# A split-fp32 decoder trunk on one core: queries, keys, attention outputs and the residual stream transposed by DMA instead of on TensorE

## The chip, the cores and the metric

The kernel runs on one core of a Trainium2 chip. The metric is device time in microseconds for one launch, the median of several runs.

## The reference

Two pre-norm layers work on 256 positions of width 2048. Cut to what matters:

```
for layer in range(2):
    xn = rms_norm(h, norm_mix)                 # h: (256, 2048)
    proj = xn @ w_in                           # 2048 x 5656: q, k, v of both head groups, gates
    o = concat(nsa_attention(...),             # 8 heads: compressed, selected and window branch
               stick_breaking_attention(...))  # 8 heads: a = exp(log_sigmoid(z) + reverse cumsum)
    h = h + (rms_norm_per_head(o) * g_grp) @ w_out
    xn = rms_norm(h, norm_ffn)
    h = h + (silu(xn @ w_gate) * (xn @ w_up)) @ w_down
return rms_norm(h, norm_final)
```

All weights and activations are float32.

## The kernel before

The weights are the bulk of the work. A planner (`plan`) writes them down once as a fixed sequence of 402 items per layer, each 128 partitions by at most 1024 columns, and the main loops go through that sequence item by item. For item `pos` a loop does three things: `step(active)` advances every piece of side work by one stage, `prefetch(pos)` lets SyncE load raw weights five tiles ahead and splits the item three places ahead into two fp32r halves (`hi` on ScalarE, L166; `lo` = raw − hi on VectorE, L167; four buffers each), and `mm(pos)` issues the item's matmuls on TensorE (L409). Each product is three passes: xh·hi, xl·hi, xh·lo. A usual item is two k-tiles by 512 columns, twelve matmuls. The item's number is thus the only clock of the program order: an instruction's place on each engine's in-order queue is the item at which its generator reached that stage.

The side work is Python generators, each `yield` of which means "one item later". `qk_chunk` takes a finished projection of queries or keys (two tiles `nat`, rows = positions), transposes them on TensorE into PSUM (L616) and copies them out on ScalarE (L617). `sb_unit` does one block of stick-breaking attention: scores `z` on TensorE, three ScalarE operations on `e`, three VectorE operations that end in `c` (L771, L773, L774), `c` = exp(c) on ScalarE (L776), then four transposes of `c` on TensorE (L780), `aT` on VectorE, and the matmuls with `sv` (L797). `nsa_unit` has a similar chain, with `pT` copied out of PSUM on ScalarE (L664). `o_norm` writes the normalised attention output `on[c]`. `xt_gen` and `xt_block` turn 512 columns of positions-by-features into the transposed and split operand `xh`/`xl`: eight TensorE transposes (L374), two VectorE multiplications by the norm's gain (L376), ScalarE `xh` (L381), VectorE `xl` (L384). They do it for the attention output (`XO`, four blocks), for the FFN's input (`X`) and for the next layer's input.

`gated`, the FFN's product, is already transposed by DMA: ScalarE copies the two tiles `sil` apart into 16-bit planes `pl` (L923), a DMA transpose, issued from ScalarE's queue, moves `pl` to `plt` (L926), four ScalarE copies put the planes together again as `sT` (L934), and `ah`/`al` are the split operand of w_down (L938, L939). The four-item pause before `sT` is written into the generator, as is one `yield` after each `pl`:

```
nc.scalar.dma_start(pt.rearrange("p t b (a s) -> p (t b a) s", a=4),
                    pl.rearrange("p t b n -> p (t b n)"), transpose=True)
for _ in range(4):
    yield
```

Of the kernel before, what the change touches and what calls it, by code (L numbers as in the profile page):

```python
# [122 lines left out]
def trunk(ctx: ExitStack, tc: tile.TileContext, x, positions, cst, gT, gfin, bgate, posT, w2, ws, out):  # L123
# [58 lines left out]
    def spawn(g):  # L182
        active.append(g)
# [5 lines left out]
    def step(lst):  # L189
        for g in list(lst):  # L190
            try:
                next(g)
            except StopIteration:
                lst.remove(g)
# [26 lines left out]
    def quad(c):  # L221
        return slice(512 * c, 512 * c + 512)
# [137 lines left out]
    def new_x():  # L360
        return [None] * 4
# [26 lines left out]
    def tmp512(name="scr"):  # L388
        return tmpp.tile([P, 512], F32, tag="scr", name=name, bufs=3)

    def xt_gen(X, c, srcs, g, ready=None):
        if ready is not None:
            while ready not in flags:
                yield
        xt_alloc(X, c)
        xt_block(X, c, srcs, g)
        yield
# [43 lines left out]
    for l in range(DEPTH):  # L441
        g_mix, g_grp, g_ffn = gt[:, 3 * l, :], gt[:, 3 * l + 1, :], gt[:, 3 * l + 2, :]
        flags.clear()
        with ExitStack() as actx:
# [152 lines left out]
            def qk_chunk(name, accs):  # L597

                sc = rq if name[0] == "q" or name[:2] == "sq" else r
                ns = []  # L600
                for t in range(2):
                    n = nat()
                    evac(n, accs[t], t, sc)
                    ns.append(n)
                yield
                if name[0] != "s":
                    for t in range(2):
                        rope(ns[t].rearrange("p (n d) -> p n d", n=4), rt, t)
                        yield
                    yield  # L610
                dst = big(name)
                dv = dst.rearrange("p (n s) -> p n s", n=4)
                for t in range(2):
                    pt = tmp_ps()
                    for j in range(4):
                        T.transpose(pt[:, j * P:(j + 1) * P], ns[t][:, j * P:(j + 1) * P], ident)  # L616
                    A.activation(dv[:, :, t * P:(t + 1) * P], pt.rearrange("p (n s) -> p n s", n=4), AF.Copy)  # L617
                    yield
                big_t[name] = dv
                flags.add(name)  # L620
# [181 lines left out]
            def sb_driver(b):  # L802
                yield from wait_for("nsa", f"sq{b}", f"sk{b}")
                yield from pipeline([sb_unit(b, 0, [0, 1, 2, 3]), sb_unit(b, 1, [0, 1]), sb_unit(b, 1, [2, 3])], 2)

            spawn(prep())
            spawn(nsa_driver())
            spawn(sb_driver(0))
            spawn(sb_driver(1))
# [1 line left out]

            ocmp = {}
            accs = None
            XO = new_x()
            while seq[pos][1].mat in ("w_in", "w_cmp_k1", "w_cmp_v1"):
                it = seq[pos][1]
                if l == 0 and pos < 6:
                    prefetch(pos)
                    step(active)
                    if pos == 3:  # L820
                        late_loads()
                else:
                    step(active)
                    prefetch(pos)
                if it.mat == "w_in":
                    for kt in it.kts:
                        while X[kt // 4] is None:
                            step(active)
                    if it.first:
                        accs = [acc(), acc()]  # L830
                    mm(pos, accs, lambda kt: X[kt // 4])
                    if it.last:
                        nm = it.name
                        if nm in ("ck", "cv"):
                            spawn(c_chunk(nm, accs))
                        elif nm == "v" or nm[:2] == "sv":
                            spawn(v_chunk(nm, accs))
                        else:
                            spawn(qk_chunk(nm, accs))
                    if it.name == "sv1" and it.kts[-1] in (3, 7, 11):  # L840
                        c = it.kts[-1] // 4
                        spawn(xt_gen(XO, c, lambda t, c=c: on[c][:, t], g_grp, f"on{c}"))
                else:
                    nm = "ck" if it.name == "wk" else "cv"
                    while nm not in flat:
                        step(active)
                    if it.first:
                        ocmp[nm] = o_ps()
                    cmp_mm(pos, ocmp[nm], flat[nm])
                    if it.last:  # L850
                        flags.add(it.name)
                        spawn(c_tail(nm, ocmp[nm]))
                parts.pop(pos)
                pos += 1
# [21 lines left out]
            while seq[pos][1].mat == "w_out":  # L876
                it = seq[pos][1]
                step(active)
                prefetch(pos)
                if it.first:  # L880
                    accs[it.name] = [acc(), acc()]
                if XO[it.kts[0] // 4] is None:
                    while f"on{it.kts[0] // 4}" not in flags:
                        step(active)
                    need(XO, it.kts[0] // 4)
                    step(active)
                    step(active)
                mm(pos, accs[it.name], lambda kt: XO[kt // 4])
                c = int(it.name[1])
                if it.last:  # L890
                    spawn(h_add(accs[it.name], c, norm))
                if c == 3 and it.kts[-1] in (1, 5, 9, 15):
                    q = it.kts[-1] // 4
                    spawn(xt_gen(X, q, lambda t, q=q: h[:, t, quad(q)], g_ffn, f"h{q}"))
                parts.pop(pos)
                pos += 1


        with ExitStack() as fctx:
# [14 lines left out]
            def gated(c, accs):  # L914


                for t in range(2):
                    s = sil[c, t]
                    V.scalar_tensor_tensor(s, accs[t], r[:, t:t + 1], s, op0=OP.mult, op1=OP.mult)  # L919
                yield  # L920
                pl = fp.tile([P, 2, 2, 512], U16, tag="pl", name="pl", bufs=1)
                for t in range(2):
                    A.activation(pl[:, t], sil[c, t].bitcast(U16).rearrange("p (n b) -> p b n", b=2), AF.Copy)  # L923
                    yield
                pt = fp.tile([P, 2, 2, 512], U16, tag="plt", name="plt", bufs=1)
                nc.scalar.dma_start(pt.rearrange("p t b (a s) -> p (t b a) s", a=4),  # L926
                                    pl.rearrange("p t b n -> p (t b n)"), transpose=True)
                for _ in range(4):
                    yield
                f = fp.tile([P, 4, S], F32, tag="sT", name="sT", bufs=1)  # L930
                fv = f.rearrange("p a s -> p (a s)").bitcast(U16).rearrange("p (a t s b) -> p t b a s", a=4, t=2, b=2)
                for t in range(2):
                    for b in range(2):
                        A.activation(fv[:, t, b], pt[:, t, b].rearrange("p (a s) -> p a s", a=4), AF.Copy)  # L934
                    yield
                ah = fp.tile([P, 4, S], F32R, tag="ah", name="ah", bufs=6)
                al = fp.tile([P, 4, S], F32R, tag="al", name="al", bufs=6)
                A.activation(ah, f, AF.Copy)  # L938
                V.tensor_tensor(al, f, ah.bitcast(F32), op=OP.subtract)  # L939
                yield  # L940
                act[c] = (ah, al)

# [37 lines left out]
            while pos < (end_at if last else len(seq)) and seq[pos][1].mat in ("w_gate", "w_up", "w_down"):  # L980
                it = seq[pos][1]
                step(active)
                prefetch(pos)
                if it.first:
                    accs = [acc(), acc()]
                src = act if it.mat == "w_down" else XF
                for kt in it.kts:
                    while src[kt // 4] is None:
                        step(active)
                mm(pos, accs, lambda kt: src[kt // 4])  # L990
                if it.last:
                    c = int(it.name[1:])
                    if it.mat == "w_down":
                        end = it.k1 == KFF
                        spawn(d_add(accs, c, end, norm))
                        if end and not last:
                            spawn(xt_gen(X, c, lambda t, c=c: h[:, t, quad(c)], gt[:, 3 * (l + 1), :], f"d{c}"))
                    else:
                        spawn(silu(c, accs) if it.mat == "w_gate" else gated(c, accs))
                parts.pop(pos)  # L1000
                pos += 1
# [94 lines left out]
```

## Time and profile before

| | |
|---|---|
| median of 3 runs | 2296.75 us (2294.84 to 2299.79) |
| the profiled execution's own time | 2295.14 us |
| its span, first to last instruction | 2293.4 us |
| mean granted TensorE clock | 0.999 |
| TensorE busy | 2269.5 us |
| VectorE busy | 1322.7 us |
| ScalarE busy | 1176.6 us |
| loads from HBM | 424.50 MB |

Busy time is summed over the instructions of an engine. All engines run beside each other and each takes its own instructions strictly in order, so an engine that is busy half the time can still hold up another one, if what the other waits for stands behind something slow in its queue.

### The profile page before, as it was taken

What the parts mean: (1) busy time and instruction counts of PE and PEld (TensorE: products, weight loads), DVE (VectorE), ACT (ScalarE), POOL (GpSimd) and SP (SyncE); (2) the same over time, 40 slices, a digit from 0 to 9 for tenths busy, and PEclk for the clock granted to TensorE, in tenths of its full rate; (3) what the DMA queues carried; (4) which work ended last, traced back from release to release, by engine and by line L of the source; (5) the groups of instructions that cost most, each with busy time, mean ns of one, the idle gap of its engine ahead of it and who ended that gap; (6) DMA issues with size and microseconds to landing.
All of it is one profiled execution on the core that took longest, in us unless ns stands there. A gap on an engine that the chain in (4) does not pass through costs nothing. (4 is left out here: it accounts for less than half of the span.)

```text
span 2293.4 us, 28108 instructions
## 1 busy us (share of the span) xinstructions
PE 2269.5 (99%) x10666; PEld 1888.1 (82%) x10666; DVE 1322.7 (58%) x1744; ACT 1176.6 (51%) x1515; POOL 28.7 (1%) x59
## 2 busy tenths in 40 slices
PE   8999999999999999999999999999999999999998
PEld 7888888888888888887888888888888888888876
DVE  6766776655545444555567667765545554445554
ACT  6645554555554345555455455545555543455543
POOL 5000000000000000000000000000000000000000
PEclk9999999999999999999999999999999999999999
DMA  7854446567677667776567434456666665566663
GB/s 252 274 174 129 124 153 199 180 204 208 201 208 203 193 193 204 209 203 191 178 215 254 147 129 143 157 186 206 213 197 210 201 203 193 195 209 202 202 193 137
DMA packets 164584, 439.98 MB, mean 192 GB/s; under 512 B 59184, under 2 KB 59600, under 8 KB 164320
## 3 DMA queue, kind: packets, MB, share of 16 engines
q1 hardware_dynamic: 118464, 426.58, 58.4%
q10 hardware_dynamic: 45760, 11.54, 3.1%
q8 instruction: 83, 1.36, 0.2%
q14 instruction: 53, 0.43, 0.1%
q0 software_dynamic: 224, 0.07, 0.0%
HBM read 424.50 MB, written 2.10 MB: 186 GB/s over the span
## 5 line engine op out<-in xcount | busy, mean ns | idle before, releaser
L167 DVE TENSOR_TENSOR lo<-raw,hi 128x1024 fp32r<-128x1024 f32 (+1 forms) x798 | 969.4, 1220 | 829.3 <-ACT hi L166 821.4
L166 ACT ACTIVATE hi<-raw 128x1024 fp32r<-128x1024 f32 (+1 forms) x798 | 835.9, 1054 | 782.4 <-PE acc L409 723.7
L409 PE MATMUL acc<-hi,xh 128*128 128x512 f32 (+2 forms) x2432 | 754.5, 391 | 0.0
L409 PE MATMUL acc<-hi,xl 128*128 128x512 f32 (+2 forms) x2432 | 738.0, 385 | 0.0
L409 PE MATMUL acc<-lo,xh 128*128 128x512 f32 (+2 forms) x2432 | 736.5, 384 | 0.0
L409 PEld LDWEIGHTS acc<-lo,xh 128*128 128x128 f32 x2432 | 452.7, 188 | 92.2 <-DVE lo L167 0.2
L409 PEld LDWEIGHTS acc<-hi,xl 128*128 128x128 f32 x2432 | 452.8, 188 | 91.8
L409 PEld LDWEIGHTS acc<-hi,xh 128*128 128x128 f32 x2432 | 444.7, 188 | 87.0 <-issue 6.7
L409 PE MATMUL acc<-hi,ah 128*128 128x512 f32 x680 | 211.1, 390 | 3.3 <-ACT ah L938 3.3
L409 PE MATMUL acc<-hi,al 128*128 128x512 f32 x680 | 211.0, 389 | 1.4 <-DVE al L939 1.4
L409 PE MATMUL acc<-lo,ah 128*128 128x512 f32 x680 | 210.7, 389 | 0.0
L409 PEld LDWEIGHTS acc<-hi,ah 128*128 128x128 f32 x680 | 127.3, 188 | 30.2 <-ACT ah L938 4.1
L409 PEld LDWEIGHTS acc<-hi,al 128*128 128x128 f32 x680 | 127.5, 188 | 28.7 <-DVE al L939 2.3
L409 PEld LDWEIGHTS acc<-lo,ah 128*128 128x128 f32 x680 | 127.7, 188 | 26.6
L934 ACT ACTIVATE sT<-plt 128x512 uint16<-128x512 uint16 x88 | 61.7, 766 | 0.0
L381 ACT ACTIVATE xh<-scr 128x512 fp32r<-128x512 f32 x48 | 29.2, 630 | 44.3 <-DVE scr L376 44.3
L664 ACT ACTIVATE pT<-tps 128x256 f32<-128x256 f32 (+1 forms) x32 | 15.7, 492 | 63.1 <-PE tps L662 63.1
L923 ACT ACTIVATE pl<-sil 128x1024 uint16<-128x1024 uint16 x44 | 46.2, 1050 | 0.0
L376 DVE TENSOR_TENSOR scr<-tps,gt 128x512 f32<-128x512 f32 x48 | 30.9, 684 | 23.3 <-PE tps L374 23.3
L919 DVE SCALAR_TENSOR_TENSOR sil<-acc,nr,sil 128x512 f32<-128x512 f32 x44 | 31.0, 747 | 13.8 <-PE acc L409 13.8
L910 ACT ACTIVATE sil<-acc,nr 128x512 f32<-128x512 f32 x44 | 27.9, 686 | 15.3 <-PE acc L409 15.3
L384 DVE TENSOR_TENSOR xl<-scr,xh 128x512 fp32r<-128x512 f32 x48 | 31.3, 692 | 5.0 <-ACT xh L381 2.9
(197 smaller groups left out, 978.5 us busy)
## 6 DMA issues: line engine op xcount, KB each, us to landing
raw<-in_ws_dram SPq DMA_DIRECT2D x792, 512.0 KB, 3.9
raw<-in_ws_dram SPq DMA_DIRECT2D x10, 420.0 KB, 5.0
h<-in_x_dram SPq DMA_DIRECT2D x3, 512.0 KB, 8.4
gf<-in_gfin_dram SPq DMA_DIRECT2D x1, 1024.0 KB, 7.2
out_dram<-h SPq DMA_DIRECT2D x4, 256.0 KB, 2.2
out_dram<-h SPq DMA_DIRECT2D x2, 512.0 KB, 3.1
cs<-in_cst_dram SPq DMA_DIRECT2D x1, 802.0 KB, 5.8
h<-in_x_dram SPq DMA_DIRECT2D x2, 256.0 KB, 4.0
```

The source lines that it names most:

```text
L166: A.activation(hi[:, :n], r[:, :n], AF.Copy)
L167: V.tensor_tensor(lo[:, :n], r[:, :n], hi[:, :n].bitcast(F32), op=OP.subtract)
L376: V.tensor_tensor(tv, pt.rearrange("p (a b) -> p a b", a=4), g[:, 4 * c:4 * c + 4, None].to_broadcast([P, 4, P]), op=OP.mult)
L381: A.activation(xh[:, :, t * P:t * P + P], ts[t], AF.Copy)
L384: V.tensor_tensor(xl[:, :, sl], ts[t], xh[:, :, sl].bitcast(F32), op=OP.subtract)
L409: T.matmul(accs[t][:, :it.w], x_[:, kt % 4, t * P:t * P + P], w_[:, sl], start=(kt == it.k0 and n == 0), stop=(kt == it.k1 - 1 and n == 2))
L664: A.activation(w[:, :nb * P], pt[:, :nb * P], AF.Copy)
L910: A.activation(s, accs[t], AF.Silu, scale=r[:, t:t + 1])
L919: V.scalar_tensor_tensor(s, accs[t], r[:, t:t + 1], s, op0=OP.mult, op1=OP.mult)
L923: A.activation(pl[:, t], sil[c, t].bitcast(U16).rearrange("p (n b) -> p b n", b=2), AF.Copy)
L934: A.activation(fv[:, t, b], pt[:, t, b].rearrange("p (a s) -> p a s", a=4), AF.Copy)
```

## The change

A generator `flip` does what the middle of `gated` did, for any pair of 512-column tiles: two ScalarE copies into 16-bit planes, a DMA transpose issued from ScalarE's queue, three items' pause, two ScalarE copies back, one more `yield`. A list `turn` admits one flip at a time, since all share one buffer of each kind. `flip_x` continues with the multiplication by the gain (VectorE) and the split into `xh` (ScalarE) and `xl` (VectorE). The list of those that now go this way, per layer: all chunks of queries and keys but `sk1` (six), three of the four blocks of `XO`, three of the four of the FFN's `X`, and in layer 0 three of the next layer's. The last block of each stays on TensorE, as does the first input. `gated` uses `flip` too, with fewer pauses and two wide copies instead of four. Flags (`used0`, `gone0`, ...) hold a new block back until the last matmuls on the old block whose buffer it takes have been issued. The buffers of a flip move to the pool of temporaries, and the area set aside for software DMA descriptors is set to 4096 bytes, which gives the room.

```diff
--- before.py
+++ after.py
@@ -388,10 +388,54 @@
     def tmp512(name="scr"):
         return tmpp.tile([P, 512], F32, tag="scr", name=name, bufs=3)
 
+    turn = []
+
+    def flip(srcs, dst):
+        while turn:
+            yield
+        turn.append(dst)
+        pl = tmpp.tile([P, 2, 2, 512], U16, tag="pl", name="pl", bufs=1)
+        for t in range(2):
+            A.activation(pl[:, t], srcs(t).bitcast(U16).rearrange("p (n b) -> p b n", b=2), AF.Copy)
+        pt = tmpp.tile([P, 2, 2, 512], U16, tag="plt", name="plt", bufs=1)
+        nc.scalar.dma_start(pt.rearrange("p t b (a s) -> p (t b a) s", a=4),
+                            pl.rearrange("p t b n -> p (t b n)"), transpose=True)
+        for _ in range(3):
+            yield
+        fv = dst().bitcast(U16).rearrange("p (a t s b) -> p t a s b", a=4, t=2, b=2)
+        for t in range(2):
+            A.activation(fv[:, t], pt[:, t].rearrange("p b (a s) -> p a s b", a=4), AF.Copy)
+        yield
+        turn.pop()
+
+    def flip_x(X, c, srcs, g, ready, slot=None):
+        while ready not in flags:
+            yield
+        f = []
+
+        def dst():
+            f.append(tmpp.tile([P, 1024], F32, tag="sT", name="sT", bufs=1))
+            return f[0]
+
+        yield from flip(srcs, dst)
+        turn.append(f)
+        fv = f[0].rearrange("p (a s) -> p a s", a=4)
+        V.tensor_tensor(fv, fv, g[:, 4 * c:4 * c + 4, None].to_broadcast([P, 4, S]), op=OP.mult)
+        while (slot is not None and slot not in flags) or (c and X[c - 1] is None):
+            yield
+        xt_alloc(X, c)
+        xh, xl = X[c]
+        A.activation(xh, fv, AF.Copy)
+        V.tensor_tensor(xl, fv, xh.bitcast(F32), op=OP.subtract)
+        turn.pop()
+        yield
+
     def xt_gen(X, c, srcs, g, ready=None):
-        if ready is not None:
-            while ready not in flags:
-                yield
+        while (ready is not None and ready not in flags) or (c and X[c - 1] is None):
+            yield
         xt_alloc(X, c)
         xt_block(X, c, srcs, g)
         yield
@@ -610,6 +654,11 @@
                     yield
                 dst = big(name)
                 dv = dst.rearrange("p (n s) -> p n s", n=4)
+                if name != "sk1":
+                    yield from flip(lambda t: ns[t], lambda: dst)
+                    big_t[name] = dv
+                    flags.add(name)
+                    return
                 for t in range(2):
                     pt = tmp_ps()
                     for j in range(4):
@@ -803,7 +852,9 @@
                 yield from wait_for("nsa", f"sq{b}", f"sk{b}")
                 yield from pipeline([sb_unit(b, 0, [0, 1, 2, 3]), sb_unit(b, 1, [0, 1]), sb_unit(b, 1, [2, 3])], 2)
 
+            XO = new_x()
             spawn(prep())
+            spawn(flip_x(XO, 0, lambda t: on[0][:, t], g_grp, "on0"))
             spawn(nsa_driver())
             spawn(sb_driver(0))
             spawn(sb_driver(1))
@@ -811,7 +862,6 @@
 
             ocmp = {}
             accs = None
-            XO = new_x()
             while seq[pos][1].mat in ("w_in", "w_cmp_k1", "w_cmp_v1"):
                 it = seq[pos][1]
                 if l == 0 and pos < 6:
@@ -837,9 +887,11 @@
                             spawn(v_chunk(nm, accs))
                         else:
                             spawn(qk_chunk(nm, accs))
-                    if it.name == "sv1" and it.kts[-1] in (3, 7, 11):
-                        c = it.kts[-1] // 4
-                        spawn(xt_gen(XO, c, lambda t, c=c: on[c][:, t], g_grp, f"on{c}"))
+                    if it.name == "sv1":
+                        if it.first:
+                            for c in (1, 2):
+                                spawn(flip_x(XO, c, lambda t, c=c: on[c][:, t], g_grp, f"on{c}", f"used{c - 1}"))
+                        flags.add(f"used{it.kts[-1] // 4 if it.kts[-1] % 4 == 3 else -1}")
                 else:
                     nm = "ck" if it.name == "wk" else "cv"
                     while nm not in flat:
@@ -885,13 +937,18 @@
                     need(XO, it.kts[0] // 4)
                     step(active)
                     step(active)
+                c = int(it.name[1])
+                if c == 2 and it.first:
+                    for q in range(3):
+                        spawn(flip_x(X, q, lambda t, q=q: h[:, t, quad(q)], g_ffn, f"h{q}",
+                                     f"gone{q - 1}" if q else None))
                 mm(pos, accs[it.name], lambda kt: XO[kt // 4])
-                c = int(it.name[1])
                 if it.last:
                     spawn(h_add(accs[it.name], c, norm))
-                if c == 3 and it.kts[-1] in (1, 5, 9, 15):
-                    q = it.kts[-1] // 4
-                    spawn(xt_gen(X, q, lambda t, q=q: h[:, t, quad(q)], g_ffn, f"h{q}"))
+                if c == 3 and it.kts[-1] % 4 == 3:
+                    flags.add(f"gone{it.kts[-1] // 4}")
+                if c == 3 and it.last:
+                    spawn(xt_gen(X, 3, lambda t: h[:, t, quad(3)], g_ffn, "h3"))
                 parts.pop(pos)
                 pos += 1
 
@@ -918,25 +975,20 @@
                     s = sil[c, t]
                     V.scalar_tensor_tensor(s, accs[t], r[:, t:t + 1], s, op0=OP.mult, op1=OP.mult)
                 yield
-                pl = fp.tile([P, 2, 2, 512], U16, tag="pl", name="pl", bufs=1)
-                for t in range(2):
-                    A.activation(pl[:, t], sil[c, t].bitcast(U16).rearrange("p (n b) -> p b n", b=2), AF.Copy)
-                    yield
-                pt = fp.tile([P, 2, 2, 512], U16, tag="plt", name="plt", bufs=1)
-                nc.scalar.dma_start(pt.rearrange("p t b (a s) -> p (t b a) s", a=4),
-                                    pl.rearrange("p t b n -> p (t b n)"), transpose=True)
-                for _ in range(4):
-                    yield
-                f = fp.tile([P, 4, S], F32, tag="sT", name="sT", bufs=1)
-                fv = f.rearrange("p a s -> p (a s)").bitcast(U16).rearrange("p (a t s b) -> p t b a s", a=4, t=2, b=2)
-                for t in range(2):
-                    for b in range(2):
-                        A.activation(fv[:, t, b], pt[:, t, b].rearrange("p (a s) -> p a s", a=4), AF.Copy)
-                    yield
+                f = []
+
+                def dst():
+                    f.append(tmpp.tile([P, 1024], F32, tag="sT", name="sT", bufs=1))
+                    return f[0]
+
+                yield from flip(lambda t: sil[c, t], dst)
+                turn.append(f)
+                f = f[0].rearrange("p (a s) -> p a s", a=4)
                 ah = fp.tile([P, 4, S], F32R, tag="ah", name="ah", bufs=6)
                 al = fp.tile([P, 4, S], F32R, tag="al", name="al", bufs=6)
                 A.activation(ah, f, AF.Copy)
                 V.tensor_tensor(al, f, ah.bitcast(F32), op=OP.subtract)
+                turn.pop()
                 yield
                 act[c] = (ah, al)
 
@@ -994,7 +1046,8 @@
                         end = it.k1 == KFF
                         spawn(d_add(accs, c, end, norm))
                         if end and not last:
-                            spawn(xt_gen(X, c, lambda t, c=c: h[:, t, quad(c)], gt[:, 3 * (l + 1), :], f"d{c}"))
+                            spawn((flip_x if c < 3 else xt_gen)(X, c, lambda t, c=c: h[:, t, quad(c)],
+                                                                gt[:, 3 * (l + 1), :], f"d{c}"))
                     else:
                         spawn(silu(c, accs) if it.mat == "w_gate" else gated(c, accs))
                 parts.pop(pos)
@@ -1082,7 +1135,7 @@
                 at += n
         arrays[f"ws{l}"] = w
 
-    nc = _bacc.Bacc("TRN2", target_bir_lowering=False, num_devices=1)
+    nc = _bacc.Bacc("TRN2", target_bir_lowering=False, num_devices=1, dynamic_dma_scratch_size=4096)
     feed, aps = {}, {}
     for name, a in arrays.items():
         feed[f"in_{name}_dram"] = a
```

What moves on the engines' queues is shown at three places of layer 0; a name in a row is a tile, and lines of the changed kernel have other numbers (its L409 is the copy out of `plt`, its matmul L453).

First, ScalarE at the end of the attention (items of `sv1`; `e` and `c` belong to `sb_unit`s, `xh` to `XO`, `hi` to the weights' split). Before:

```order
L767 ACTIVATE e<-tps 128x512
L768 ACTIVATE e<-e 128x512
L769 ACTIVATE e<-e 128x512
L381 ACTIVATE xh<-scr 128x4x128 x2
L166 ACTIVATE hi<-raw 128x1024 x2
L776 ACTIVATE c<-c 128x512
L767 ACTIVATE e<-tps 128x512
L768 ACTIVATE e<-e 128x512
L769 ACTIVATE e<-e 128x512
L381 ACTIVATE xh<-scr 128x4x128 x2
L166 ACTIVATE hi<-raw 128x1024 x2
```

With the change, from the same `sb_unit` on:

```order
L816 ACTIVATE e<-tps 128x512
L817 ACTIVATE e<-e 128x512
L818 ACTIVATE e<-e 128x512
L409 ACTIVATE sT<-plt 128x4x256 x2
L166 ACTIVATE hi<-raw 128x1024
L431 ACTIVATE xh<-sT 128x1024
L401 ACTIVATE pl<-on_2750 128x1024 x2
L403 DMA_TRANSPOSE plt<-pl 128x16x128
L166 ACTIVATE hi<-raw 128x1024
L825 ACTIVATE c<-c 128x512
L816 ACTIVATE e<-tps 128x512
L817 ACTIVATE e<-e 128x512
```

Between the `e` of one unit and its `c` there stood the two short `xh` and two splits; now there stand the copies of one flip, the split, that flip's `xh`, and the planes and the issue of the next flip.

Second, VectorE at the same place. Before:

```order
L167 TENSOR_TENSOR lo<-raw,hi 128x1024 x2
L376 TENSOR_TENSOR scr<-tps,gt 128x512 x2
L384 TENSOR_TENSOR xl<-scr,xh 128x4x128 x2
L167 TENSOR_TENSOR lo<-raw,hi 128x1024
L771 SCALAR_TENSOR_TENSOR e<-tps,e 128x512
L773 SCALAR_TENSOR_TENSOR c<-cs,e 128x512
L774 TENSOR_TENSOR c<-tps,c 128x512
L167 TENSOR_TENSOR lo<-raw,hi 128x1024
L376 TENSOR_TENSOR scr<-tps,gt 128x512 x2
L384 TENSOR_TENSOR xl<-scr,xh 128x4x128 x2
```

With the change:

```order
L167 TENSOR_TENSOR lo<-raw,hi 128x1024 x5
L820 SCALAR_TENSOR_TENSOR e<-tps,e 128x512
L822 SCALAR_TENSOR_TENSOR c<-cs,e 128x512
L823 TENSOR_TENSOR c<-tps,c 128x512
L426 TENSOR_TENSOR sT<-sT,gt 128x1024
L432 TENSOR_TENSOR xl<-sT,xh 128x1024
L167 TENSOR_TENSOR lo<-raw,hi 128x1024 x2
L836 TENSOR_TENSOR aT<-tps,cs 128x512
L820 SCALAR_TENSOR_TENSOR e<-tps,e 128x512
L822 SCALAR_TENSOR_TENSOR c<-cs,e 128x512
L823 TENSOR_TENSOR c<-tps,c 128x512
```

The multiplication by the gain is one wide instruction on `sT` behind `c`, in the place of two short ones on PSUM, and `xh` on ScalarE comes after it.

Third, ScalarE in the items of `o2` and `o3` of the output projection (`h` is the residual stream, L347 its squares). Before:

```order
L347 ACTIVATE scr,nss<-h 128x512 x2
L166 ACTIVATE hi<-raw 128x1024 x2
L347 ACTIVATE scr,nss<-h 128x512 x2
L166 ACTIVATE hi<-raw 128x1024 x8
L347 ACTIVATE scr,nss<-h 128x512 x2
L381 ACTIVATE xh<-scr 128x4x128 x2
L166 ACTIVATE hi<-raw 128x1024 x2
L381 ACTIVATE xh<-scr 128x4x128 x2
```

With the change:

```order
L347 ACTIVATE scr,nss<-h 128x512 x2
L166 ACTIVATE hi<-raw 128x1024 x2
L347 ACTIVATE scr,nss<-h 128x512 x2
L401 ACTIVATE pl<-h 128x1024 x2
L403 DMA_TRANSPOSE plt<-pl 128x16x128
L166 ACTIVATE hi<-raw 128x1024 x3
L409 ACTIVATE sT<-plt 128x4x256 x2
L166 ACTIVATE hi<-raw 128x1024
L431 ACTIVATE xh<-sT 128x1024
L401 ACTIVATE pl<-h 128x1024 x2
L403 DMA_TRANSPOSE plt<-pl 128x16x128
L166 ACTIVATE hi<-raw 128x1024 x3
```

The `xh` of a block and the planes and the issue for the next block now follow one another with no split between them.

## Rows read from the trace of the kernel before

**Rows 1.** the page's busy line, and its line of the ScalarE DMA queue

```profile
PE 2269.5 (99%) x10666; PEld 1888.1 (82%) x10666; DVE 1322.7 (58%) x1744; ACT 1176.6 (51%) x1515; POOL 28.7 (1%) x59
...
q10 hardware_dynamic: 45760, 11.54, 3.1%
```

**Rows 2.** waits of TensorE: us in total, times, longest us

```profile
PE acc L409 <- ACT ah L938: 3.3, 2, 1.6
...
PE acc L409 <- DVE al L939: 1.4, 2, 0.7
```

**Rows 3.** TensorE's timeline, 280 to 284 us: start, us, instruction

```profile
280.08 0.62 PE L409 MATMUL acc<-lo,xh 128*128 128x512 f32 x2
280.54 0.60 PE L616 MATMUL tps<-cs,nat 128*128 128x128 f32 x4
...
283.29 0.61 PE L409 MATMUL acc<-lo,xh 128*128 128x512 f32 x2
```

**Rows 4.** groups by line, TensorE transposes: busy us, mean ns, idle before

```profile
L374 PE MATMUL tps<-cs,h 128*128 128x128 f32 x128 | 20.0, 303 | 9.8 <-DMA cs<-in_cst_dram 4.1 <-DMA h<-in_x_dram 3.4 <-DVE scr L376 1.7
...
L616 PE MATMUL tps<-cs,nat 128*128 128x128 f32 x112 | 16.9, 274 | 0.0
...
L374 PE MATMUL tps<-cs,on 128*128 128x128 f32 x64 | 8.7, 274 | 0.4 <-DVE c L774 0.4
```

**Rows 5.** the tile plt: durations ns min/median/max, and landing

```profile
L926 ACTq DMA_TRANSPOSE plt<-pl x22: 1333/3644/4919, 476.1 to 2177.8; - x22
...
DMA to landing us min/median/max: 5.3/7.4/9.6
```

**Rows 6.** ScalarE's timeline, 560 to 580 us, behind one DMA transpose

```profile
567.30 2.24 ACT L166 ACTIVATE hi<-raw 128x1024 fp32r<-128x1024 f32 x2 [3.16 <-issue]
571.19 1.06 ACT L166 ACTIVATE hi<-raw 128x1024 fp32r<-128x1024 f32 x1 [1.65 <-PE acc L409]
573.91 1.06 ACT L166 ACTIVATE hi<-raw 128x1024 fp32r<-128x1024 f32 x1 [1.66 <-PE acc L409]
```

**Rows 7.** groups by line, the pieces of a flip and of a split

```profile
L167 DVE TENSOR_TENSOR lo<-raw,hi 128x1024 fp32r<-128x1024 f32 (+1 forms) x798 | 969.4, 1220 | 829.3 <-ACT hi L166 821.4 <-PE acc L409 6.6
L166 ACT ACTIVATE hi<-raw 128x1024 fp32r<-128x1024 f32 (+1 forms) x798 | 835.9, 1054 | 782.4 <-PE acc L409 723.7 <-issue 30.9 <-ACT pl L923 15.7
...
L923 ACT ACTIVATE pl<-sil 128x1024 uint16<-128x1024 uint16 x44 | 46.2, 1050 | 0.0
```

**Rows 8.** ScalarE's timeline, 315 to 346 us

```profile
317.89 0.63 ACT L769 ACTIVATE e<-e 128x512 f32<-128x512 f32 x1
...
324.39 0.63 ACT L776 ACTIVATE c<-c 128x512 f32<-128x512 f32 x1 [2.93 <-DVE c L774]
```

**Rows 9.** VectorE's timeline, the same stretch

```profile
330.60 0.68 DVE L771 SCALAR_TENSOR_TENSOR e<-tps,e 128x512 f32<-128x512 f32 x1
331.32 1.22 DVE L773 TENSOR_TENSOR_SCAN c<-cs,e 128x512 f32<-128x512 f32 x1
```

**Rows 10.** TensorE's timeline, the transposes of c in that stretch

```profile
327.66 0.60 PE L780 MATMUL tps<-cs,c 128*128 128x128 f32 x4
...
334.50 0.60 PE L780 MATMUL tps<-cs,c 128*128 128x128 f32 x4
...
342.43 0.66 PE L780 MATMUL tps<-cs,c 128*128 128x128 f32 x4
```

**Rows 11.** ScalarE's timeline, 225 to 300 us

```profile
277.13 0.63 ACT L769 ACTIVATE e<-e 128x512 f32<-128x512 f32 x1
```

**Rows 12.** TensorE's timeline, the same stretch

```profile
284.63 0.60 PE L780 MATMUL tps<-cs,c 128*128 128x128 f32 x4
```

**Rows 13.** waits of all engines: us in total, times, longest us

```profile
ACT pT L664 <- PE tps L662: 63.1, 32, 2.8
```

**Rows 14.** TensorE's timeline from 86 us, one item of the compression

```profile
86.09 0.28 PE L539 MATMUL ops<-hi,fr 128*60 128x256 f32 x1
...
86.79 0.28 PE L539 MATMUL ops<-hi,fr 128*60 128x256 f32 x1
```

## The prediction

> **What bounds the kernel now.** I read the page's busy line first: TensorE works 2269.5 of 2293.4 us, VectorE 1322.7 and ScalarE 1176.6 [rows 1]. So time falls only if TensorE gets less work, and rises with each new wait of TensorE. Its waits came second, by their releaser: beside the start the only ones on this change's path are 3.3 + 1.4 us at the second part of w_down, for `ah` and `al`, the end of `gated`'s chain [rows 2]. Third came the timelines, since the change puts its work on ScalarE, half idle but in order: what counts is not its total but what stands behind a flip. Two cadences matter. A usual item lasts 2.72 us (two splits gated by TensorE start at 571.19 and 573.91, [rows 6]). A split may start when the item four places before it has left its buffer, three items ahead of its use; `hi` takes 1.05 and `lo` 1.22 us [rows 7].
>
> **What the change removes.** 96 of the 112 transposes of queries and keys, 72 of the 128 of `h` (the 32 of the first input stay) and 48 of the 64 of `on` [rows 4]: 216. Their listed means of 0.27 to 0.30 us overlap, so I take their pitch. From 280.08 to 283.29 there are six pairs of matmuls and four transposes in 3.21 us [rows 3]; six pairs are an item, 2.72; the rest is 0.49, or 0.1225 each. 216 make **26.5 us** less of TensorE. `gated`'s shorter chain (two yields fewer) should end the waits for `ah` and `al`: **4.7 us** [rows 2]. Gains: 31.2 us.
>
> **What a flip costs.** Two `pl` copies at 1.05 us [rows 7]; two copies back of the same number of 16-bit elements, priced the same, 2.1 us together; for `flip_x` a wide multiplication, priced as `lo`, 1.22, and `xh`, priced as `hi`, 1.05. The unknown is how long the issue holds ScalarE. The 22 issues of before last 1.33 to 4.92 us, median 3.64 [rows 5]; behind one of them ScalarE's next split waited 3.16 us "for issue" [rows 6]. I take 3.0 us, a little under the middle, and keep 1.33 and 4.92 as bounds. From issue to landing it is 5.3 to 9.6, median 7.4 us [rows 5], against a pause of three items, 8.2. There are 27 more flips, 15 in layer 0 and 12 in layer 1; the three extra are the next layer's input.
>
> The Trainium skill, "VectorE: DVE Perf Modes", The three transpose paths, speaks against such a trade: 1309 ns for one 128x128 block by DMA, and 390 on TensorE. By it the 16 blocks of a flip would land after 21 us (an estimate), 12.8 beyond the pause, and 27 times that less the gain would end near 2610 us. The trace does not agree: 16 blocks land in 7.4 us, 0.46 each [rows 5], and TensorE's transpose costs 0.1225 in pitch.
>
> **Where the cost is hidden.** In the FFN the planes, the issue, `hi` and `lo` are 2.1 + 3.0 + 1.05 + 1.22 = 7.4 us against a lead of 8.2 and another 0.9 until `lo` is used in an item's third pass; the 22 flips of `gated` hang on nothing shorter. The same goes for `qn0` and the next layer's input, whose flips are items apart: 0. With 4.92 it is 9.3 against 9.1, 0.2 for a few: left out.
>
> **End of the attention (XO1, XO2), per layer.** Here a `c` on ScalarE is wanted by TensorE soon, and it stands behind a flip. The three `e` end at 318.52 [rows 8]. With the change then come, each waiting for the one before: `sT` 2.1, `hi` 1.05, `lo` 1.22, on VectorE the chain to `c` 0.68 + 1.22 + 0.68 [rows 9], the multiplication 1.22, `xh` 1.05, next planes 2.1, issue 3.0, `hi` 1.05, and `c` itself 0.63 [rows 8]: 16.0, ends 334.5. Before, `c` ended at 325.02 [rows 8], and TensorE took it at 327.66 [rows 10]; without 16 transposes (1.96) it wants it at 325.7. Late 8.8. The second `c`: from there 3 `e` 1.9, `hi` 1.05, `lo` 1.22, `aT` (0.68, a form like `e`'s) and chain 3.26, `c` 0.63: 8.1 us, where TensorE had 334.50 - 327.66 = 6.84 less eight transposes, 5.9: late 2.2. The third: `e` 1.9, `sT` 2.1, `sv` 0.63, `hi` 1.05, `lo` 1.22, `aT` and chain 3.26, multiplication 1.22, `xh` 1.05, `hi` 1.05, the output's copy 0.63, `c` 0.63: 14.7 against 342.43 - 334.50 = 7.9 [rows 10]: late 6.8. Together **17.8** (bounds 16.1 and 19.7, by the issue alone).
>
> **Output projection (X0 to X2).** Take the start of the item in whose step X0's `sT` stands as zero. Its planes, three items before and behind one split, are done at -7.7, so they land at -0.3. Then `sT` 2.1, `hi`, `lo` 2.27, multiplication 1.22, `xh` 1.05, planes 2.1, issue 3.0, `hi`, `lo` 2.27: 14.0, ends 13.7. That `lo` is for the item at 4 x 2.72, third pass, 11.8: late 1.9. X1's planes are done at 8.4, land at 15.8; the same 14.0, two squares and one more `hi` make 16.3, ends 32.1, due at 9 x 2.72 + 0.9 = 25.4. In all **6.7** late (about 2.9 if issues are 1.33 and landings 5.3; 10 with 4.92 and 9.6).
>
> **The flip of k.** It falls among the short items of the compression, eight matmuls at a pitch of (86.79 - 86.09)/6 = 0.117, 0.93 us each [rows 14]. 7.4 us of planes, issue and split against a lead of three such, 2.8: **4.6** (2.9 to 6.5).
>
> **The flip of sq1.** `e` ends at 277.76 [rows 11]; planes 2.1, issue 3.0, `hi`, copy, `hi`, `c` 3.4: 286.2. TensorE took `c` at 284.63 [rows 12], now 0.49 earlier: **2.1** (0.5 to 4.0).
>
> **Flips beside NSA (qn1, sq0, sk0, XO0).** ScalarE waits 63.1/32 = 2.0 us for TensorE before each `pT` [rows 13], and TensorE wants each within an item or so. Planes and issue are 5.1; where one such gap takes it (sk0) 3.1 is late, where two do, 1.1, three times: **6.4** (1.4 to 14).
>
> **Sum.** 17.8 + 6.7 + 4.6 + 2.1 + 6.4 = 37.6 per layer, 75 in two, less 31.2: +44 on the profiled 2295.14, which lies 1.6 under the median of 2296.75, inside its runs. **2339 us.** Bounds together: 23.6 a layer, 2311; 54.2, 2372.
>
> **Rivals.** *The flips are hidden* (0.15): ScalarE is 49% idle, so only the gains show: 2295.1 - 31.2 = 2264. Against it, `c` ended only 2.6 us before it was taken, and one issue alone is 3. It decides if the issue does not hold ScalarE, and the waits for `sT`'s multiplication fit in the idle time before `c` (2.93, [rows 8]).
>
> *The issue is short* (0.2): 1.33 us, as the shortest of before, in each new flip: 2311. Against it, the median of 22 of the same size was 3.64 [rows 5]. The Trainium skill, "DMA: Bandwidth & Descriptors", Issuing engines are not separate DMA queues, has the time to initiate a DMA as usually small relative to the DMA; rows 5 show the half of it, 3.64 of 7.4.
>
> *Loads become the bound* (0.04): the transposes' queue took 3.1% of 16 engines over the span [rows 1], 71/22 = 3.2 us each; if 27 more pushed the loads back by that, 87 - 31 = +56, 2351. Against it: 22 such transposes ran beside loads already, and beyond the start I found no wait of TensorE for a load.
>
> *Losses and gains cancel* (0.09): the lateness in one place leaves slack for the next (after a stall all splits are early), so half of the 75 remains, near 2300.
>
> **How the numbers follow.** The forecast's own case has 0.52, with 2311 to 2372. What this kernel's measurement can tell from no change is 0.2%, 4.6 us. Faster: the hidden case and a third of the cancelled, 0.18; same: half of the cancelled, 0.05; slower 0.77. The range is 2295 to 2372: below it lies the hidden case, above it some 0.04.
>
> **What would show it.** Right: TensorE's busy time some 26 us less and its share near 96 to 97%; new waits of TensorE for `c` and for `hi`/`lo`, about 8 us where the first of the `c` behind XO1's flip is due; 49 issues of 1.3 to 4.9 us with more of ScalarE's waits "for issue" [rows 6]; the waits for `ah` and `al` gone. Wrong: issues that leave ScalarE running, multiplications that VectorE does before `c`, or splits so early that a late one meets no wait; then the span shrinks by up to 31 us.

## The result and the profile after

The changed kernel takes 2323.55 us in the median of 4 runs (2320.13 to 2324.17), the kernel before 2296.64 us beside it: 1.0113 times as long, 95% interval 1.0095 to 1.013. It is slower, by 27 us; 2339 with 2295 to 2372 was forecast.

The page of the changed kernel, its busy line and ScalarE's DMA queue [rows 1]:

```profile
span 2322.0 us, 27668 instructions
...
PE 2263.3 (97%) x10450; PEld 1875.2 (81%) x10450; DVE 1312.2 (57%) x1714; ACT 1252.9 (54%) x1540; POOL 29.2 (1%) x59
...
q10 hardware_dynamic: 101920, 25.70, 6.1%
```

TensorE runs 216 matmul instructions less, but its busy time fell by 6 us only, and the time in which it is idle went from 2293.4 - 2269.5 = 24 us to 59. Two things need an explanation: what it waits for, and why the busy time fell so little. The waits of TensorE in the changed kernel [rows 2] answer the first:

```profile
PE tps L829 <- ACT c L825: 18.7, 4, 7.6
PE ops L846 <- ACT on L761: 10.0, 2, 5.0
...
PE tps L374 <- DVE h L916: 2.2, 2, 1.1
PE tps L747 <- DVE pc L744: 2.0, 2, 1.1
PE ops L846 <- DVE aT L832: 2.0, 2, 1.3
PE ops L584 <- DVE lo L167: 1.9, 2, 0.9
PE ops L583 <- ACT hi L166: 1.8, 2, 1.1
```

The waits for `ah` and `al` are gone. Those for `c` and for the output copy `on` are new and the largest, four and two in number: a few places, the same in both layers. ScalarE's timeline at the larger wait for `c` in layer 0 [rows 8]:

```profile
321.63 0.63 ACT L818 ACTIVATE e<-e 128x512 f32<-128x512 f32 x1
322.17 2.24 ACT L409 ACTIVATE sT<-plt 128x1024 uint16<-128x1024 uint16 x2
324.31 1.04 ACT L166 ACTIVATE hi<-raw 128x1024 fp32r<-128x1024 f32 x1
330.42 1.06 ACT L431 ACTIVATE xh<-sT 128x1024 fp32r<-128x1024 f32 x1 [5.07 <-DVE sT L426]
331.39 1.99 ACT L401 ACTIVATE pl<-on 128x1024 uint16<-128x1024 uint16 x2
333.40 1.33 ACTq L403 DMA_TRANSPOSE plt<-pl  x1
334.84 1.06 ACT L166 ACTIVATE hi<-raw 128x1024 fp32r<-128x1024 f32 x1 [1.47 <-issue]
335.80 0.61 ACT L825 ACTIVATE c<-c 128x512 f32<-128x512 f32 x1
```

VectorE's timeline beside it:

```profile
325.38 1.23 DVE L167 TENSOR_TENSOR lo<-raw,hi 128x1024 fp32r<-128x1024 f32 x1 [5.32 <-ACT hi L166]
...
328.51 0.69 DVE L823 TENSOR_TENSOR c<-tps,c 128x512 f32<-128x512 f32 x1
329.11 1.22 DVE L426 TENSOR_TENSOR sT<-sT,gt 128x1024 f32<-128x1024 f32 x1
```

The order is the one put on record for the queues. ScalarE stands idle for 5.07 us before `xh`, until a multiplication is done that stands behind `lo` and `c`'s own chain on VectorE; and `c`, whose input was ready as that multiplication began, waits for `xh`, the planes, the issue and a split. TensorE's timeline there [rows 10] shows what that costs and, behind it, the second answer:

```profile
328.78 0.61 PE L453 MATMUL acc<-lo,xh 128*128 128x512 f32 x2
336.47 1.11 PE L829 MATMUL tps<-cs,c 128*128 128x128 f32 x4 [7.07 <-ACT c L825]
337.23 1.20 PE L453 MATMUL acc<-hi,xh 128*128 128x512 f32 x2
338.23 1.05 PE L453 MATMUL acc<-hi,xl 128*128 128x512 f32 x2
...
343.68 0.62 PE L453 MATMUL acc<-hi,xl 128*128 128x512 f32 x2
```

After 7.07 us of waiting a pair of matmuls takes 1.05 us and not 0.62. The stretches of that place (busy us by engine, then the granted clock, DMA share, GB/s):

```profile
328.00:330.00 2.00, 1.40 (x7) 0.80 (x5) 1.97 (x3) 0.00 (x0) 0.00 (x0) 1.00 0.66 250
...
332.00:334.00 2.00, 0.00 (x0) 0.00 (x0) 0.73 (x1) 1.37 (x2) 0.00 (x0) 0.50 0.00 0
...
340.00:342.00 2.00, 2.00 (x6) 1.59 (x5) 1.97 (x4) 0.12 (x1) 0.00 (x0) 0.50 0.28 70
342.00:344.00 2.00, 2.00 (x10) 1.65 (x9) 1.97 (x3) 0.35 (x1) 0.00 (x0) 0.96 0.54 217
```

The granted clock falls to its lower level (0.50, 1.2 of 2.4 GHz) while TensorE waits and returns some 6 us after it works again. The wait for `on` has the same cause, an `xh` that stands on ScalarE in front of the copy and waits for its multiplication, and the same dip of the clock behind it:

```profile
355.43 1.06 ACT L431 ACTIVATE xh<-sT 128x1024 fp32r<-128x1024 f32 x1 [5.67 <-DVE sT L426]
356.39 1.04 ACT L166 ACTIVATE hi<-raw 128x1024 fp32r<-128x1024 f32 x1
357.34 0.58 ACT L761 ACTIVATE on<-ops 128x512 f32<-128x512 f32 x1
```

```profile
357.97 2.07 PE L846 MATMUL ops<-sv,aT 128*128 128x128 f32 x8 [5.01 <-ACT on L761]
```

Through the lower clock a part of what the waits cost is counted as busy time, and that hides part of the saving.

The issues were shorter than taken, as was the landing [rows 5]:

```profile
L403 ACTq DMA_TRANSPOSE plt<-pl x49: 1332/1939/4677, 83.6 to 2207.1; - x49
...
DMA to landing us min/median/max: 4.2/5.4/8.9
```

### The profile page after: what moved, and what is told of

Its sections match the earlier page's. It is cut to its first block, busy times and chain, and to the rows that moved or that the text cites. A ratio compares the mean times of both kernels' runs of the same rounds, so it can differ in the third digit from the quotient of the medians.

```text
span 2322.0 us, 27668 instructions
## 1 busy us (share of the span) xinstructions
PE 2263.3 (97%) x10450; PEld 1875.2 (81%) x10450; DVE 1312.2 (57%) x1714; ACT 1252.9 (54%) x1540; POOL 29.2 (1%) x59
## 4 chain that ended last, share of the span: by engine, by line
PE 87%; ACT 6%; DVE 4%; ACTq 1%; issue 1%; DMA 0%; SPq 0%; DVEq 0%
PE acc L453 82%; ACT hi L166 2%; DVE lo L167 1%; ACTq L403 1%; ACT sT L409 1%; ACT pl L401 1%; PE ops L719 1%; PE tps L690 1%; DVE c L822 1%; PE ops L583 1%; PE ops L584 1%; DVE sT L426 1%; ACT xh L431 0%; DMA raw<-in_ws_dram 0%; PE tps L711 0%
## 5 line engine op out<-in xcount | busy, mean ns | idle before, releaser
L453 PE MATMUL acc<-hi,xh 128*128 128x512 f32 (+2 forms) x2432 | 758.8, 393 | 0.2
L453 PE MATMUL acc<-hi,xl 128*128 128x512 f32 (+2 forms) x2432 | 742.1, 387 | 0.0
L453 PE MATMUL acc<-lo,xh 128*128 128x512 f32 (+2 forms) x2432 | 739.6, 385 | 0.6 <-DVE lo L167 0.5
L453 PEld LDWEIGHTS acc<-lo,xh 128*128 128x128 f32 x2432 | 454.7, 189 | 95.6 <-DVE lo L167 3.0
L453 PEld LDWEIGHTS acc<-hi,xl 128*128 128x128 f32 x2432 | 455.2, 189 | 93.0
L453 PEld LDWEIGHTS acc<-hi,xh 128*128 128x128 f32 x2432 | 448.4, 189 | 90.7 <-issue 7.6
L453 PE MATMUL acc<-hi,al 128*128 128x512 f32 x680 | 210.7, 389 | 0.0
L453 PE MATMUL acc<-lo,ah 128*128 128x512 f32 x680 | 210.6, 389 | 0.0
L453 PE MATMUL acc<-hi,ah 128*128 128x512 f32 x680 | 210.6, 389 | 0.0
L453 PEld LDWEIGHTS acc<-lo,ah 128*128 128x128 f32 x680 | 127.6, 188 | 26.5
L453 PEld LDWEIGHTS acc<-hi,al 128*128 128x128 f32 x680 | 127.6, 188 | 26.5
L453 PEld LDWEIGHTS acc<-hi,ah 128*128 128x128 f32 x680 | 127.6, 188 | 26.5
L409 ACT ACTIVATE sT<-plt 128x1024 uint16<-128x1024 uint16 x74 | 83.0, 1169 | 0.5 <-DMA plt<-pl 0.5
L431 ACT ACTIVATE xh<-sT 128x1024 fp32r<-128x1024 f32 x15 | 15.9, 1060 | 44.2 <-DVE sT L426 44.2
L583 PE MATMUL ops<-hi,fr 128*60 128x256 f32 x128 | 31.9, 282 | 1.8 <-ACT hi L166 1.8
L584 PE MATMUL ops<-lo,fr 128*60 128x256 f32 x128 | 31.5, 280 | 1.9 <-DVE lo L167 1.9
L347 ACT ACTIVATE scr<-h 128x512 f32<-128x512 f32 x38 | 23.8, 627 | 13.0 <-DVE h L1002 9.7
```

The costliest lines, as they stand in the source:

```text
L347: A.activation(scr, h[:, t, quad(c)], AF.Square, accum_out=self.ss[:, t, c:c + 1])
L409: A.activation(fv[:, t], pt[:, t].rearrange("p b (a s) -> p a s b", a=4), AF.Copy)
L453: T.matmul(accs[t][:, :it.w], x_[:, kt % 4, t * P:t * P + P], w_[:, sl], start=(kt == it.k0 and n == 0), stop=(kt == it.k1 - 1 and n == 2))
L583: T.matmul(o[:60, :256], fr[:, kt, :], hi[:, sl], start=(kt == 0), stop=False)
L584: T.matmul(o[:60, :256], fr[:, kt, :], lo[:, sl], start=False, stop=(kt == 31))
```

## Experiments

Theory A is the prediction's: the loss sits where a latency chain of ScalarE stands behind a flip, most of all behind those of XO1 and XO2. Theory B is the rival that every flip costs about the same, by its DMA traffic. Theory C says that it is the issue alone, in which ScalarE stands still. The kernel before took 2296.8 to 2297.1 us beside these runs.

**XO1 and XO2 back on TensorE.**

```diff
-                        if it.first:
-                            for c in (1, 2):
-                                spawn(flip_x(XO, c, lambda t, c=c: on[c][:, t], g_grp, f"on{c}", f"used{c - 1}"))
+                        if it.kts[-1] in (7, 11):
+                            c = it.kts[-1] // 4
+                            spawn(xt_gen(XO, c, lambda t, c=c: on[c][:, t], g_grp, f"on{c}"))
```

> XO1 and XO2 go back to TensorE transposes, the other flips stay. Theory A (the loss sits at the end of the attention, where c and the output copy stand behind a flip on ScalarE, and in the lower clock after these two waits): the two waits of 7.1 to 7.6 and 5.0 us per layer and the clock's 5.3 us per layer go, 32 transposes at 0.1225 us come back: 2323.6 - 24.7 - 10.6 + 3.9 = 2292 us, granted clock 0.997 or more. Theory B (each of the 27 flips costs about the same 2.1 us, by DMA traffic and issue): 2323.6 - 4 x 2.1 + 3.9 = 2319 us.

Measured: 2293.22 us (2292.35 to 2294.03), 0.9983 of before (0.9973 to 0.9992), clock 0.997. B, which gave 2319, is out: four flips of 27 carry 30 us. The wait for `c` that is left in its list belongs to `sq1`'s flip:

```profile
PE tps L829 <- ACT c L825: 4.1, 2, 2.0
...
PE ops L846 <- DVE aT L832: 2.5, 2, 1.3
```

**XO1 and XO2 alone by DMA.** The other 23 flips go back to TensorE, as in the next experiment.

> gated's change and the flips of XO1 and XO2 alone, the other 23 on TensorE. Theory A: from 2292 the two waits and the clock's part, + 24.7 + 10.6, less 32 transposes, 3.9: 2323 us, nearly all of the loss with 4 of 27 flips. Theory B: 2292 + 4 x 2.1 - 3.9 = 2297 us.

Measured: 2320.83 us (2320.40 to 2321.61), 1.0104 (1.0090 to 1.0118). Its waits are those two again:

```profile
PE tps L829 <- ACT c L825: 16.6, 2, 8.8
PE ops L846 <- ACT on L761: 10.4, 2, 5.2
```

**gated's change alone.** The XO, X and next-layer blocks and all of q and k use the TensorE path; the moved buffers and the smaller descriptor area stay. Of the edit, the line for q and k:

```diff
-                if name != "sk1":
+                if name not in ('k', 'qn0', 'qn1', 'sq0', 'sk0', 'sq1', 'sk1'):
```

> Only gated's shorter chain, with shared buffers and the smaller descriptor area; all 27 new flips go back to TensorE. All theories: the waits for ah and al go, 4.7 us: 2292 us; 2297 if something later takes their place.

Measured: 2289.40 us (2289.18 to 2290.89), 0.9968 (0.9955 to 0.998), 7.4 us less. Of it 4.7 are the waits that were forecast; in the profiled execution a wait for `scr` of 1.7 is gone too. TensorE's busy time is 2269.5 as before, so nothing came from its work. What of the 7.4 belongs to the buffers and the descriptor area was not tried apart.

**xh one item later.** In every `flip_x`, cut to the place:

```diff
         V.tensor_tensor(fv, fv, g[...], op=OP.mult)
+        yield
         while (slot is not None and slot not in flags) or ...:
```

> One yield more between the multiplication by the gain and xh in every flip_x; c then stands ahead of xh, the planes and the issue on ScalarE's queue. Nothing is taken out. Theory A, with the wait of xh for VectorE (5.1 and 5.7 us) as its main part: the first c no longer waits for mult, xh, planes and issue, 1.2 + 5 + 1.06 + 2 + 1.5 us less some 2 for its own chain: both waits of TensorE shrink to under 2 us and the clock stays up there: about 2293 us. Theory B: 2323 us. Theory C (the issue, which holds ScalarE, is what costs): the issue is moved only behind c, c2 then waits: 2310 us or more.

Measured: 2304.21 us (2303.09 to 2305.34), 1.0032 (1.0019 to 1.0044). The mechanism holds, for the same instructions in another order take 19 us less; the size does not (A gave 2293, C 2310 or more). TensorE's timeline of this kernel says why:

```profile
328.57 0.66 PE L830 MATMUL tps<-cs,c 128*128 128x128 f32 x4 [0.52 <-ACT c L826]
...
340.80 1.11 PE L830 MATMUL tps<-cs,c 128*128 128x128 f32 x4 [5.20 <-ACT c L826]
```

The first `c` is on time within 0.52 us and the wait for `on` is gone, but `xh`, planes and issue, 4.4 us, now stand in front of the split and so of the second `c`, which is 5.20 late. A wait moved to the next link of the chain.

**Issue from SyncE.** All 49 transposes, those of `gated` too; the arguments are cut:

```diff
-        nc.scalar.dma_start(pt.rearrange(...), pl.rearrange(...), transpose=True)
+        nc.sync.dma_start(pt.rearrange(...), pl.rearrange(...), transpose=True)
```

> All 49 DMA transposes are issued from SyncE's queue instead of ScalarE's; SyncE carries only the loads, whose next one waits for a split that stands behind the planes anyway. Theory A (what delays c is the whole row of pieces in front of it, of which the issue is 1.3 of 14 us): the first c 1.4 us earlier, k's wait 1.4 and sq1's 1.9 us less, each twice: 2323.6 - 9 = 2314 us. Theory C (the issue, which holds ScalarE, is what costs): the 73 us of ScalarE's waits for issue are gone, and with them most of the new waits of TensorE: 2295 us or less.

Measured: 2301.90 us (2301.15 to 2302.84), 1.0021 (1.0012 to 1.003). Between A's 2314 and C's 2295: the issue is worth 21.7 us, more than A gave it. In the two profiles TensorE's idle time is 13.5 us less, and its busy time, for the same 10450 matmul instructions, 9.2 less (2254.1), at a mean granted clock of 0.994 for 0.990. The waits for `pc`, `aT` and the compression's `hi` are gone, those for its `lo` and for `h` are 0.3 and 0.6 us in all; the two largest remain. ScalarE's waits "for issue" in front of `hi` fall from 73.4 to 31.8 us and not to nothing, so that word in a row is not the DMA issue alone. The waits:

```profile
PE tps L829 <- ACT c L825: 13.9, 4, 5.5
PE ops L846 <- ACT on L761: 10.4, 2, 5.2
```

So C explains most of the small waits, and 1.6 of the 7.1 us at the first `c`; it does not explain `on`, where the 5.66 us wait of `xh` for the multiplication is unchanged.

**Matmuls into the wait.** 28 matmuls with an unused result, so that TensorE does not idle in front of the first `c` of the second half, in each layer:

```diff
+                if b == 1 and qi == 0:
+                    for _ in range(28):
+                        T.matmul(pt, X[3][0][:, 0, 0:P], parts[min(parts)][0][:, 0:512], start=True, stop=True)
                 for j in range(4):
                     T.transpose(pt[:, j * P:(j + 1) * P], c[:, j * P:(j + 1) * P], ident)
```

> The changed kernel with 28 extra matmuls (128x512, results unused) put ahead of the transposes of the first c of the second half in each layer: at 0.227 us each 6.4 us of work in the 7.1 us wait. Theory A's clock part: TensorE no longer idles there, the granted clock stays at its upper level behind it, and the about 5.7 us of work that ran at the lower one are 2.9 us shorter, in two layers 5.7: 2318 us, though the added work is 12.7 us. If the low clock were not due to the wait: 2324 us, and a dip of the same length in the same place.

Measured: 2323.99 us (2321.22 to 2327.03), no gain, where 2318 was expected. The clock's half of the expectation came true. TensorE's timeline and the stretches of this kernel:

```profile
328.69 6.51 PE L830 MATMUL tps<-hi,xh 128*128 128x512 f32 x28
335.92 0.66 PE L832 MATMUL tps<-cs,c 128*128 128x128 f32 x4 [0.72 <-ACT c L825]
...
343.79 0.66 PE L832 MATMUL tps<-cs,c 128*128 128x128 f32 x4 [0.83 <-ACT c L825]
...
348.31 1.16 PE L849 MATMUL ops<-sv,aT 128*128 128x128 f32 x8 [1.11 <-ACT sv L527]
```

```profile
332.00:335.00 3.00, 3.00 (x15) 2.31 (x13) 0.20 (x1) 1.54 (x2) 0.00 (x0) 1.00 0.33 65
335.00:338.00 3.00, 2.28 (x12) 1.81 (x12) 1.23 (x1) 2.94 (x6) 0.00 (x0) 1.00 0.72 131
...
356.00:359.00 3.00, 1.58 (x7) 1.59 (x8) 2.47 (x3) 3.00 (x5) 0.00 (x0) 0.50 0.00 0
```

The clock stays at its upper level behind the filled wait and falls, in this stretch, only at the unfilled one for `on`, at 356. But a TensorE that is quicker there waits 0.83 for the second `c` and 1.11 for `sv`, which it did not before. The chain through ScalarE and VectorE sets that place; the slow clock after the first wait was covered by it and cost nothing that shows.

**Flips where neither `c` nor the compression stands behind them.** XO1, XO2, k and sq1 on TensorE, the other 19 flips kept.

> Flips only where neither c nor the compression stands behind them: XO1, XO2, k and sq1 back on TensorE, 19 flips and gated's change stay. From gated_only's 2289.4: 64 transposes of qn0, qn1, sq0, sk0, 16 of XO0, 48 of X and 24 of the next layer's input at 0.094 us each (the pitch of all removed ones in the two traces) are 14.3 less, the waits left in xo_pe for pc and h are 4.5 more: 2280 us by theory A. Theory B (each flip costs 2.1 us): 2289.4 + 19 x 2.1 - 14 = 2315 us.

Measured: 2280.69 us (2279.50 to 2281.54), 0.9929 (0.9916 to 0.9943). It beats both kernels, as A forecast (2280; by B 2315), and its list has no wait of TensorE for ScalarE's `c`.

**Both remedies.** XO1 and XO2 on TensorE, the 23 others and `gated` by DMA from SyncE:

> XO1 and XO2 on TensorE, the other 23 flips (k and sq1 too) by DMA, all transposes issued from SyncE. Theory A (what is left outside XO1 and XO2 was the issue in front of c, the compression, pc and h): these waits are under 0.6 us each as in sp_issue, so from best's 2280.7: 32 transposes of k and sq1 at 0.094 us and the 3.8 us of waits for pc and h less: 2274 us. If the 2.1 us of copies, not the issue, made k and sq1 costly: 2281 us or more.

Measured: 2275.30 us (2274.92 to 2275.46), 0.9904 (0.9890 to 0.9919), the best of all: 22 us under the kernel before, 48 under the change. The busy line of its page, and its only wait of TensorE behind a flip that is longer than 0.6 us:

```profile
PE 2250.7 (99%) x10482; PEld 1869.3 (82%) x10482; DVE 1317.2 (58%) x1722; ACT 1239.9 (55%) x1528; POOL 28.9 (1%) x59
```

```profile
PE tps L829 <- ACT c L825: 2.9, 2, 1.5
```

**All flips, issue from SyncE, xh later.**

> All 27 flips, issued from SyncE, and xh one item behind the multiplication. Theory A: the second c, 5.2 us late with the late xh, is 1.4 us earlier without the issue, the output's copy does not wait for the multiplication: about 3.8 us left per layer, against 5.5 + 5.2: 2301.9 - 2 x 6.9 = 2288 us. If the multiplication in front of xh hides nothing: 2302 us.

Measured: 2283.68 us (2283.38 to 2284.83), 0.9943 (0.9926 to 0.9959), 4 us less than expected. Even with XO1 and XO2 by DMA the change then wins. What is left is in the main the second `c` again, at most 3.7 us late:

```profile
PE tps L830 <- ACT c L826: 11.3, 6, 3.7
```

## Why the prediction was right, point by point

**The sign and the place: right.** It said that a half-idle, in-order ScalarE would make TensorE wait at `c`, most of all behind XO1 and XO2, and that this costs more than the transposes give.

**XO1 and XO2, 17.8 us a layer: right in the sum.** The two cuts give it: 2323.55 - 2293.22 = 30.3, and 2320.83 - 2289.40 = 31.4, each with 32 transposes more or less at 0.1 us; so 33.6 and 34.7 us, against 35.6 in two layers. The first piece came out as its working has it: 7.07 for the first `c` where it gave 8.8, less the 1.67 by which the issue was shorter (1.33 for 3.0). The second `c`, 2.2 in the sum, shows no wait, because TensorE came to it slowly; the matmuls put into the first wait made one of 0.83 appear, and 1.11 for `sv`. The third term showed as the wait for `on`, 5.0 for 6.8, with the low clock behind it. That the sums lie so near is in part luck: with the issue as measured its own working gives 16.1 a layer, and the lower clock, for which it has no term, makes up the difference. Between the kernels with gated's change alone and with XO1 and XO2 added, TensorE's idle time grows by 26.7 us; another 7.5 are busy time (2273.7 for 2269.5, with 32 transposes less).

**The other flips, 19.8 us a layer: the mechanism right, the size twice too large.** From 2289.40 to 2293.22 the 23 other flips lose 3.8 us, and their 184 transposes gave 18.8 (TensorE's busy time 2269.5 in the kernel with gated's change alone, 2250.7 in the one with both remedies): 22.6 us in all, for 39.6. Some 16 of it is idle time, and 5.3 is busy time at a lower clock (2256.0 with the issue on ScalarE, 2250.7 with it on SyncE, for the same 10482 instructions). The step that was mis-sized is "I take 3.0 us" for the issue and 7.4 for the landing: the median issue is 1.94 and the landing 5.4. In the output projection, 6.7 in the sum, that left 1.1 per layer, and at another place: TensorE waits for `h` in front of the last block's transposes, and for no `lo` of w_out. For `k` it left 1.9 of 4.6, beside NSA 1.0 (`pc`) of 6.4. Only sq1 cost more than the 2.1 given: 1.3 for an `aT`, then 2.0 for `c`, and a dip of the clock. There the sum ran from the splits straight to `c`; in the trace ScalarE idles 3.05 us in between for VectorE, which has `lo`, `aT` and the chain to `c` still to do.

**The gains, 31.2 us: near.** The busy time gives 18.8/184 = 0.102 us a transpose for the 0.1225 worked out of one place, so 22 for 216 and not 26.5; `gated` gave 7.4 for 4.7; its chain is four `yield`s shorter, not two: two in front of the issue and two behind it. Together: 34 + 22.6 - 22 - 7.4 = +27. That this is the measured difference proves nothing by itself, since the costs were taken from the same runs.

**The rivals.** "The flips are hidden" is what the kernel with both remedies comes nearest to, 2275 against 2264, with two blocks a layer left on TensorE. "The issue is short", 2311, was nearer on the issue, at XO1 even exact, and still 12 us low. It has the pieces around the issue in it; what it lacks is the median of 1.94 for its 1.33, sq1, the clock, and gains that came out smaller by 2. (Its lower bounds add up to 23.8 a layer and not 23.6, which changes it by less than 0.5 us.) By the Trainium skill's rule beside it ("DMA: Bandwidth & Descriptors", Issuing engines are not separate DMA queues) the issue would be small beside the transfer; the trace does not agree, 1.94 of 5.4 us, and taking it off ScalarE was worth 21.7. That loads become the bound did not happen: the splits on ScalarE waited 4.8 us for loads before and 6.7 with the change, and 3.5 to 8.1 in the other kernels. "Losses and gains cancel", near 2300, took half of the 75 us of costs; 56 came.

**Clock.** The prediction had no term for it, and its sign of TensorE's busy time some 26 us less failed mainly by it: 6 us. The matmuls behind each long wait are longer at the lower clock; whether this adds to the time was tried for the first wait only, where it did not. Behind the wait for `on` no further wait of TensorE follows within 80 us in layer 0 that could take it up, so there it probably adds; no run tries it alone.

## What to carry to other kernels

An engine that is half idle is not free: work put into an in-order queue costs what stands behind it, so read the latency chains (here `e`, `c`, transpose, `aT`) and price each new piece by the next link's due time, not by the engine's busy share. Split a helper so that the part that waits for another engine comes a stage later, and issue its DMA from a queue that has nothing more urgent (here SyncE's loads, which did not become the bound); then look which link of the chain is late next. Some places are best left alone: with the issue on SyncE 23 of 27 flips win 14 us (2289.4 to 2275.3, `gated`'s own issue moved along), and with the last four added these are lost and more (2301.9); with `xh` later as well the four cost 8 (2283.7).

## What the runs showed of the hardware

The same DMA transpose of 128x2048 16-bit elements held ScalarE's queue from 1.33 to 4.68 us in one execution, and from SyncE's queue 1.32 to 4.35 (median 3.31):

```profile
L403 SPq DMA_TRANSPOSE plt<-pl x49: 1322/3310/4352, 82.7 to 2184.6; - x49
```

What sets it stays open. TensorE's granted clock was 0.50 in the latter part of a 7 us wait and for some 6 us after it, and 1.00 throughout where matmuls filled the same wait.
